# A hybrid attention layer on one core: the mixers' table of steps, reordered over 240 positions

## The chip, the cores and the metric

The kernel runs on one core of one Trainium2 chip. The metric is the device time of one execution in microseconds (us). Three runs of the kernel before the change took 1100.43, 1100.59 and 1101.66 us, so their median is 1100.59 us. One more execution was profiled: it took 1101.76 us, and its span from the first to the last recorded instruction is 1100.0 us. All durations below come from that one.

## The reference

One decoder layer on 512 tokens of width 1024, in float32:

```
h  = x + 1/2 * SwiGLU_1(RMSNorm(x))                  # feed-forward width 2816
u  = RMSNorm(h);  columns of u @ w_in (1024 x 3992): q, k, v of two attentions, branch gates, two merge gates
A  = native sparse attention: compressed keys + selected blocks + window 512; 8 heads of 64, 2 key/value groups
B  = sliding-window attention, window 128, 8 heads, one key/value group, one sink per head
h  = h + w_out( sigmoid(gA) * (A @ w_branch_a) + sigmoid(gB) * (B @ w_branch_b) )
h  = h + 1/2 * SwiGLU_2(RMSNorm(h));  out = RMSNorm(h)
```

The compressed keys and values are a small network over blocks of 32 tokens, `gelu(block @ w1) @ w2`, one for keys and one for values.

## The kernel before, in words

Every large product keeps its precision by splitting both operands into a high part (rounded to the fast matmul type) and a low part (what is left), and by adding three products: high x high, high x low, low x high. So each block of weights, 128 x 1024 numbers that the SP queue loads into `raw`, passes through ScalarE (ACT), which writes `whi` (line 151), and then through VectorE (DVE) or GpSimd (POOL), which writes `wlo` = raw - whi (line 155). Four blocks of `raw` and four of `whi`/`wlo` exist at a time; the load of a block four places ahead is issued behind the second half of a block's low part.

The program runs in stages: the first feed-forward net, the two mixers (attentions A and B), the merge, the second feed-forward net, the last norm. Only the mixers are touched. There the program is cut into 1123 small tasks, in `plan`. Each task is a handful of instructions on one engine:

- `project`: one of 8 groups of six matmuls (line 387, `acc`) that fill one of two accumulator banks with a piece of u @ w_in. What drains the bank (rope on DVE, lines 1166 and 1169; value halves on ACT and DVE, line 1231) sets it free.
- `rope_tasks`, `q_done`, `kv_done`: rotation of queries and keys. Two DVE passes from the bank, an add of the two halves (line 1184, DVE or POOL), then for queries a high part on ACT (line 1260), a low part (line 1263, DVE or POOL), and four transposes on TensorE (line 1272, `tp`), copied out by ACT (line 1277).
- `compress`: four groups of matmuls, a sum on DVE (line 1374), `sums` on TensorE, a polynomial on DVE (lines 1387 to 1389), tanh on ACT, a product on DVE (line 1396), a second product on TensorE (`second`, line 387 `tp<-w,sqacc`), and so on.
- `attend`: for each unit of 128 queries, scores on TensorE (`s`), mask and minimum on DVE (line 1551, with a small add in line 1555), exponentials on ACT (line 1559), the inverse of the sums on DVE (a small add in line 1568 and a reciprocal in line 1569), the weighting (line 1580, DVE or POOL), transposes on TensorE (line 1645), their high part on ACT (line 1657) and low part on DVE (line 1660), the value products, and the sum of two halves (line 1688).
- `prepare`: the high (line 151) and low (line 155) half of a block of weights; the low one on DVE or POOL.

`follow` (in `Schedule`) walks through the table `ORDER`, a list of task numbers, and lets each task write its instructions. Each engine then executes its own instructions strictly in that order and waits by semaphores for what the others make; no engine passes over a waiting instruction. For a task that may run on DVE or POOL, a `p` behind its number puts it on POOL. At every 64th position of the table (63, 127, 191, 255 in the part concerned) `follow` also issues one DMA on POOL's queue, which sums weights for the second feed-forward net in memory. So the table fixes three things: the order on TensorE, ACT, DVE and POOL, which of DVE and POOL does a task, and where POOL's DMAs and SP's loads of weights stand.

Of the kernel before, what the change touches and what calls it, by code (L numbers as in the profile page):

```python
# [207 lines left out]
def cols(w, width, r0, nk, c0, n):  # L208
# [4 lines left out]


ORDER = """
    0 1 2 3 4 5 6 7 14 15 16 10 11p 13 17 32 8 18 36 33 19 37 20 9 21 34 12 44 38 40 80 48 35 41 49 42 23 22 50 39p
    24 26 51 52 25p 53 43p 27 86 54 84 55 45 64 29 82 65 46 30 66 81 85 83p 67 56 57p 68 69 28 31 47 58 87 70 71 59
    72 88 93 95 94p 96 89 60 61 62 90 97 98 91 99 489 100 101 133 134 102 137 135 73 138 139 136 103 104 92 74 63
    140p 105 490 106 75p 502 107 503 108 117 78 491 109 118 76 119 77 492 504 110 507 120 111 493 121 112 122 505 79
    494 506 495 123 496 113 124 155 157 524 115 161 508 141 142 114 125 497 156p 525 143 159 158p 160p 144 163 145  # L220
    498 195 162 146 164 126 199 147 509 526 165 166 197 196p 200 116 167 168 198p 148 510 169 170 149 150 127 499
    176 128p 151 201 529 172 202p 129 500 173p 152 177 130 131 178 511 153 175 154 179 171 132 512 501 527 180 530
    513 528p 516 181 174 517 514 182 183 531 518 185 208 210 212 209 211 213 546 184 515 203 519 187 186p 204 205
    214 551 520 206 547 216 521 217 248 215p 218 249p 188 252 192 219 220 250 253p 552 522 548 193 221 532 189 254
    549 190 523p 251 207 194 222 553 191 223 255p 232 233 533 534 550p 538 234 554 224 535 568 225p 536 539 537 235
    226 540 541 569 542 555p 236 570 543 237 227 238 571 544 545 556 557 560 239 572 561 256 269 240 257 258 271
    270p 273 558 581 259 309 586 313 228 275 260 562 559 272p 261 311 274p 277 582 229 278 262 563 230 564 231 587
    276p 263 279 280 565 312p 281 241p 310p 573 583 603 264 282 574 588 265 584 314p 283 608 266 604 267 605 284
    585p 268 290 291 315 316p 566 285 567p 589 292 575 609 610 606 576 242 286 243p 577 293 294 288 295 611 296 578
    590 244 607 579 246 245 297 360 247 298 591 580 317 595 592 612 299 625 630 318 301 596 287p 289 300p 593 319  # L230
    597 626 302 303 594 306 598 304 307 627 599 305 308 320 613 631 321 614 349 617 618 322 632 600 615 619 323 601
    324 616 602 628 620 325 333 621 334 335 629p 622 633 336 623 326 337 634 338 327 339 635 340 328p 636 329 624p
    350 637 371 330 341 639 640 331 647 342p 332 638 343 641 642 648 656 351 344p 352 657 353 345 643 644 354 649
    347 650 346 665 355 658 651 652 666 348 677 659 356 357 682 653 654 667 660p 668 678 661 645 358 662 655 361 669
    670 663 362 363 664 671 683 672 679 695 684 680 696 364 365 697 685 646p 700 366 701 681p 367 698 686p 687 673
    359 702 368 674 703 713 393 725 691 699p 714 369 688 372 675 689 692 693 373 726 690 370 382 704p 715 705 716
    706 707 730 727 676 694 374 728 729p 709 735 717 708 710 375 711 731 718 719 712 732 376 720 740 736 721 737 741
    733 742 377 722 378 738 757 743 379 739p 758 762 380 734p 759 763 383 384 744p 767 760 745 764 768 746 749 404
    765 772 761p 750 747 385 386 769 770 753 415 748 751 723 754 724p 789 771p 773 752 755 387 774 790 801 756 791
    775 802 766p 806 388 776p 777 781 807 389 803 778 811 390 782 381 792 779 808 785 783 780 812 391 784 804 805p  # L240
    786 793 392 809 813 787 794 394 814 815p 810p 795 816 837 817 788 796 838 395 426 396 797 818 798 397 842 819
    820 839 843 840 847 799 848 800p 821 822 825 398 841p 826 823 399 844 849 829 824 852 827 828 830 833 834 845
    873 400 853 850 854 851p 831 835 832 401 874 846p 855 836 875 856p 885 405 857 406 858 876 859 861 407 865 862
    886 890 860 863 887 866 891 867 869 402 864 888 870 408 871 892 877 895 868 900 896 409 893 897 872 901 921 898
    902 410 878 903 922 411 923 879 926 412 894p 924 416 880 899p 417 904p 931 889 881 905 909 927 882 925p 932 928
    936 906 418 910 419 413 907 911 929 908 930p 933 883 934 913 937 448 914 917 915 912 957 918 420 919 916 437
    935p 938 969 939 958 403 970 421 974 940p 941 920 975 959 960 942 945 971 946 422 943 423 979 949 972 947 976
    977 944 980 950 951 948 984 978p 953 981 427 985 952 982 954 986 961 428 962 1001 429 955 983p 1006 987 956 884p
    988p 963 964 1002 424 973p 1003 965 989 1007 1011 990 430 993 966 1008 991 1012 425 994 1009 431 997 992 998
    1013 432 1016 995 996 1033 1004 999 433 967 1005p 434 1017 1018 1010p 1014 1034 1035 1045 1015p 1019 1020 459  # L250
    1000 1021 1025 968p 1046 1036 1022 1026 438 1023 439 1050 1029 1024 1047 414 1030 1027 1051 1037 1048 1031 1028
    1052 440 1053 1032 1049p 1063 441 1054p 1038 1039 1064 1040 442 1068 435 1041 1065 1042 1055 1069 1056 1059 443
    1060 1066 1070 1057 1061 444 1081 1058 445 1082 481 1093 1067p 449 1071 1083 1072p 1102 1073 1043 1077 1094 1095
    450 451 1084 1062 1103 1074 1096 485 1044p 452 1097p 1078 1075 1111 1085 1104 1079 1112 1105 436 1076 1086 1087
    1106p 1113 1080 1098 453 454 455 1088 1107 446 456 482p 1114 1089 1099 1108 483 1109 460 470 461 462 463 464
    1100 1090 465 1101 1091 1092p 457 486p 466 1115 1110 447 467 1116 487 471 1117 1118 472 1119 484p 488p 1120 1121
    458 473 474 475 476 477 478 479 468 1122p 480 469
"""


# [1894 lines left out]
```

## Time and profile before

| what | value |
|---|---|
| three runs | 1100.43, 1100.59, 1101.66 us |
| profiled execution / its span | 1101.76 / 1100.0 us |
| TensorE busy (PE) | 1085.4 us, 99% of the span |
| VectorE busy (DVE) | 756.5 us, 69% |
| ScalarE busy (ACT) | 526.4 us, 48% |
| GpSimd busy (POOL) | 212.5 us, 19% |
| mean granted TensorE clock | 0.997 |

The mixers' tasks start at 378.6 us of the span; position 60 of the table lies at 398.3 us and position 298 at 460.1 us. In a row of a timeline the first number is the start, the second the duration, and the bracket tells how long the engine was idle before it and what ended that; an "x3" merges equal neighbours. In a row of waits stand the total, the count and the longest. In a row of windows stand, after the stretch, the busy time of PE, PEld, DVE, ACT and POOL with instruction counts, the granted TensorE clock, the DMA share and GB/s.

### The profile page before, as it was taken

How to read it: one execution, taken by the hardware profiler on the slowest of the kernel's cores; microseconds unless marked ns; L12 is line 12 of the kernel's file. 1: busy time of each engine (PE TensorE's matmuls, PEld its weight loads, DVE VectorE, ACT ScalarE, POOL GpSimd, SP SyncE). 2: the span in 40 equal slices, each digit the busy share in tenths (PEclk: the TensorE clock that was granted, in tenths of full speed). 3: DMA queues.
4: the chain of work that ended last, by engine and by line, in shares of the span. 5: the costliest groups of instructions: out<-in, count | busy, mean ns of one | idle time of the engine just before them, and what ended most of it. 6: DMA issues, size and time to landing. Idle time of an engine off the chain costs nothing.

```text
span 1100.0 us, 15779 instructions
## 1 busy us (share of the span) xinstructions
PE 1085.4 (99%) x5835; PEld 934.1 (85%) x5835; DVE 756.5 (69%) x1356; ACT 526.4 (48%) x966; POOL 212.5 (19%) x245
## 2 busy tenths in 40 slices
PE   9999999999999999999999999999999999999997
PEld 7888899988888999998888888888888888888886
DVE  5665778864556578897777657655678867787673
ACT  5433335433334455776767634444335445554442
POOL 0311220000001135565443522122100000000002
PEclk9999999999999999999999999999999999999999
DMA  7989988698756536446969676637998864646622
GB/s 217 259 211 230 250 199 231 207 291 293 229 193 193 143 116 194 153 140 159 301 192 364 149 195 183 191 96 192 245 263 244 264 192 156 191 153 192 211 77 77
DMA packets 203205, 220.90 MB, mean 201 GB/s; under 512 B 7700, under 2 KB 160088, under 8 KB 202840
## 3 DMA queue, kind: packets, MB, share of 16 engines
q1 hardware_dynamic: 177208, 156.84, 45.4%
q0 software_dynamic: 23456, 58.72, 23.2%
q10 hardware_dynamic: 2464, 4.33, 1.1%
q8 instruction: 46, 0.75, 0.3%
q14 instruction: 31, 0.25, 0.1%
HBM read 199.94 MB, written 78.64 MB: 253 GB/s over the span
## 4 chain that ended last, share of the span: by engine, by line
PE 91%; DVE 5%; ACT 1%; issue 1%; DMA 1%; POOLq 0%; ACTq 0%; DVEq 0%
PE acc L387 29%; PE o L387 20%; PE s L387 20%; PE o L1872 4%; PE o L786 3%; PE acc L1872 3%; PE s L1872 3%; PE tp L1645 2%; PE s L786 2%; PE acc L786 2%; DVE wlo L155 1%; DMA raw<-in_ffn_down_dram 1%; DVE s L1551 1%; DVE turn_a L1344 0%; ACT whi L151 0%
## 5 line engine op out<-in xcount | busy, mean ns | idle before, releaser
L155 DVE TENSOR_TENSOR wlo<-raw,whi 128x1024 fp32r<-128x1024 f32 (+2 forms) x219 | 256.5, 1193 | 62.9 <-ACT whi L151 62.4
L151 ACT CAST whi<-raw 128x1024 fp32r<-128x1024 f32 (+2 forms) x244 | 222.0, 935 | 90.0 <-PE acc L387 12.4
L387 PE MATMUL acc<-uh,whi 128*128 128x512 f32 x240 | 96.2, 401 | 0.0
L387 PE MATMUL acc<-uh,wlo 128*128 128x512 f32 x240 | 93.9, 391 | 0.0
L387 PE MATMUL acc<-ul,whi 128*128 128x512 f32 x240 | 93.7, 390 | 0.0
L387 PE MATMUL acc<-whi,uh 128*128 128x256 f32 x224 | 65.9, 294 | 1.3 <-ACT whi L151 1.3
L387 PE MATMUL acc<-wlo,uh 128*128 128x256 f32 x224 | 63.6, 284 | 0.1
L387 PE MATMUL acc<-whi,ul 128*128 128x256 f32 x224 | 63.6, 284 | 0.0
L387 PE MATMUL o<-uh,whi 128*128 128x512 f32 x144 | 57.4, 399 | 0.6 <-ACT whi L930 0.6
L1660 DVE TENSOR_TENSOR pts<-tp,pts 128x512 fp32r<-128x512 f32 (+1 forms) x62 | 41.9, 687 | 22.7 <-ACT pts L1657 21.8
L387 PE MATMUL o<-ul,whi 128*128 128x512 f32 x144 | 56.2, 390 | 0.0
L387 PE MATMUL o<-uh,wlo 128*128 128x512 f32 x144 | 56.1, 390 | 0.0
L387 PEld LDWEIGHTS acc<-uh,wlo 128*128 128x128 f32 x240 | 45.1, 188 | 10.2 <-DVE wlo L155 0.4
L387 PEld LDWEIGHTS acc<-ul,whi 128*128 128x128 f32 x240 | 45.2, 188 | 8.1
L387 PEld LDWEIGHTS acc<-uh,whi 128*128 128x128 f32 x240 | 45.1, 188 | 8.0
L1559 ACT ACTIVATE pbuf<-s,m 128x256 f32<-128x256 f32 (+3 forms) x96 | 47.5, 503 | 8.4 <-DVE m L1551 4.0
L387 PE MATMUL acc<-G,whi 128*128 128x512 f32 x164 | 50.5, 389 | 0.0
L387 PE MATMUL s<-uh,whi 128*128 128x512 f32 x128 | 49.9, 390 | 0.0
L387 PE MATMUL s<-ul,whi 128*128 128x512 f32 x128 | 49.8, 389 | 0.0
L387 PE MATMUL s<-uh,wlo 128*128 128x512 f32 x128 | 49.8, 389 | 0.0
L2050 POOL TENSOR_TENSOR o_t<-o_t,g_b 128x512 f32<-128x512 f32 (+1 forms) x5 | 5.9, 1181 | 227.3 <-ACT z L2044 227.3
L387 PE MATMUL s<-G,whi 128*128 128x512 f32 x160 | 49.4, 390 | 0.0
(468 smaller groups left out, 2923.3 us busy)
## 6 DMA issues: line engine op xcount, KB each, us to landing
raw<-in_ffn_gate_dram SPq DMA_DIRECT2D x42, 512.0 KB, 4.8
raw<-in_ffn_down_dram SPq DMA_DIRECT2D x34, 512.0 KB, 5.1
raw<-in_ffn_up_dram SPq DMA_DIRECT2D x32, 512.0 KB, 6.8
t<-in_ffn_down_dram POOLq DMA_DIRECT2D x12, 1024.0 KB, 9.7
w<-in_ffn_up_dram POOLq DMA_DIRECT2D x12, 1024.0 KB, 11.5
raw<-w SPq DMA_DIRECT2D x24, 512.0 KB, 4.2
raw<-in_w_in_dram SPq DMA_DIRECT2D x20, 512.0 KB, 4.5
raw<-s SPq DMA_DIRECT2D x16, 512.0 KB, 4.9
```

Source lines behind the costliest of these rows:

```text
L151: self.nc.scalar.copy(self.place(i)[0][:, k0:k1], self.raw[i][:, k0:k1])
L155: engine.tensor_tensor(lo, self.raw[i][:, k0:k1], f32(hi), op=OP.subtract)
L387: tensor.matmul(out, lhsT, rhs, start=start, stop=stop)
L786: tensor.matmul(o, a_[:, n], x(k), start=new and n == step == 0, stop=n == 7 and step == 2, skip_group_check=True)
L1551: vector.tensor_tensor_reduce(b.view[:, j], b.view[:, j], u.mask, 1.0, u.least(hd), OP.add, OP.min, u.m[:, hd:hd + 1])
L1559: scalar.activation(u.p[:, hd], b.view[:, j], AF.Exp, bias=u.m[:, hd:hd + 1], scale=-1.0, accum_out=u.sum[:, hd:hd + 1])
L1645: tensor.transpose(ps[:w, hd], u.p[:, hd, kb * w:kb * w + w], ident)
L1660: vector.tensor_tensor(p.lo, flat(b.ps)[:w], f32(p.hi), op=OP.subtract)
L1872: tensor.matmul(ps, x, y[:, k], start=new and kk == k == step == 0, stop=kk == k == 1 and step == 2, skip_group_check=True)
L2050: gpsimd.tensor_tensor(y, y, left["g_b"][:, cs], op=OP.mult)
```

## The change

Positions 60 to 297 of `ORDER` are written anew; all before and behind is the same. The same tasks stand there, none is added or removed, and TensorE and ACT get the same 90 and 62 tasks in another order. 19 tasks change between DVE and POOL: 12 go to POOL (seven low halves of weights in line 155; one low part in line 1350; one in line 1263; two weightings of two heads in line 1580; one output low part in line 1693), and 7 go to DVE (two low halves of weights, three rope adds in line 1184, two weightings). DVE has 59 tasks there instead of 64, POOL 27 instead of 22. The table takes one line more, so that every later line number is one larger in the changed kernel. The diff, cut to its first lines:

```diff
-    24 26 51 52 25p 53 43p 27 86 54 84 55 45 64 29 82 65 46 30 66 81 85 83p 67 56 57p 68 69 28 31 47 58 87 70 71 59
-    72 88 93 95 94p 96 89 60 61 62 90 97 98 91 99 489 100 101 133 134 102 137 135 73 138 139 136 103 104 92 74 63
...
+    39p 24 26 51 52 25p 53 43p 27 86 54 84 55 45 64 29 82 65 46 30 66 28 83 81p 56 85p 87 67 68 57 69 70 31 58
+    59 71 93 60 61 47p 62 88 63 72 89 90 73 91 489 94p 95 74 96 101 102 92 97 98 502 75p 99 100 76 77 103 104
...
```

Three places show how the instructions move. The first is DVE at position 60, from the last piece of the compression's input (line 1344, shown as the first row) to the low part of the first query (line 1263), which TensorE's transposes in line 1272 wait for. Before:

```order
L1344 TENSOR_TENSOR turn_a<-tp,cols_c 64x8x31 x4
L155 TENSOR_TENSOR wlo<-raw,whi 128x512 x2
L1166 TENSOR_TENSOR turn_a<-acc,cos 128x512
L1169 TENSOR_TENSOR turn_b<-acc,sin 128x8x32 x2
L1314 TENSOR_SCALAR gate<-gate 128x96
L1315 RECIPROCAL gate<-gate 128x96
L1195 SCALAR_TENSOR_TENSOR ks_t<-tp,ks_t 128x512
L1350 TENSOR_TENSOR G<-turn_a,G 128x16x32
L155 TENSOR_TENSOR wlo<-raw,whi 128x512
L1263 TENSOR_TENSOR ql<-turn_a,ql 128x8x64
```

and in the changed kernel:

```order
L1345 TENSOR_TENSOR turn_a<-tp,cols_c 64x8x31 x4
L1315 TENSOR_SCALAR gate<-gate 128x96
L1316 RECIPROCAL gate<-gate 128x96
L155 TENSOR_TENSOR wlo<-raw,whi 128x512
L1167 TENSOR_TENSOR turn_a<-acc,cos 128x512
L1170 TENSOR_TENSOR turn_b<-acc,sin 128x8x32 x2
L155 TENSOR_TENSOR wlo<-raw,whi 128x512
L1185 TENSOR_TENSOR turn_a<-turn_a,turn_b 128x512
L1196 SCALAR_TENSOR_TENSOR ks_t<-tp,ks_t 128x512
L1264 TENSOR_TENSOR ql<-turn_a,ql 128x8x64
```

One low half and the low part of line 1350 have left DVE for POOL, and the rope add of line 1184 has come to it from there. On POOL the low half, the DMA and the rope add that stood here have become a low half, the DMA, a second low half and the low part. On TensorE the transposes now stand right behind the projection's last group, ahead of the first two groups of the compression, which stood ahead of them.

The second place is DVE between the compression's polynomial (its last row is line 1389, in the changed kernel 1390) and its product (line 1396, now 1397), which TensorE's second product waits for. Before:

```order
L1389 SCALAR_TENSOR_TENSOR sqacc<-sqacc,tp 128x128
L155 TENSOR_TENSOR wlo<-raw,whi 128x512
L1568 TENSOR_TENSOR sum<-sum,e 128x2
L1569 RECIPROCAL c<-sum 128x2
L1396 SCALAR_TENSOR_TENSOR sqacc<-sqacc 128x128
```

and in the changed kernel, from the low half on:

```order
L155 TENSOR_TENSOR wlo<-raw,whi 128x512
L1185 TENSOR_TENSOR turn_a<-turn_a,turn_b 128x512
L1569 TENSOR_TENSOR sum<-sum,e 128x2
L1570 RECIPROCAL c<-sum 128x2
L1552 ISA s,m<-s,mask_s,sink 128x256
L1552 ISA m 128x1
L1552 ISA s,m<-s,mask_s,sink 128x256
L1552 ISA m 128x1
L1556 TENSOR_TENSOR e<-m,sink 128x2
L1397 SCALAR_TENSOR_TENSOR sqacc<-sqacc 128x128
```

The low half here belongs to another half of the weights than the one before (that one is now on POOL); a rope add and the minima of two heads have come between, and two more heads' minima stand between polynomial and low half (not shown).

The third place is DVE behind the rope passes over the first half of the second key/value projection (lines 1166 and 1169). Before:

```order
L1169 TENSOR_TENSOR turn_b<-acc,sin 128x4x32 x2
L155 TENSOR_TENSOR wlo<-raw,whi 128x512 x3
L1231 SCALAR_TENSOR_TENSOR v<-acc,rcol,v 128x2x64 x2
L1551 ISA s,m<-s,mask_s,sink 128x256
L1551 ISA m 128x1
```

and in the changed kernel:

```order
L1170 TENSOR_TENSOR turn_b<-acc,sin 128x4x32 x2
L1552 ISA s,m<-s,mask_s,sink 128x256
L1552 ISA m 128x1
L1552 ISA s,m<-s,mask_s,sink 128x256
L1552 ISA m 128x1
L1556 TENSOR_TENSOR e<-m,sink 128x2
L1232 SCALAR_TENSOR_TENSOR v<-acc,rcol,v 128x2x64 x2
L155 TENSOR_TENSOR wlo<-raw,whi 128x512 x3
```

The value halves (line 1231), which free the accumulator bank, now stand ahead of the three low halves, with the minima of two heads ahead of them.

More of the change, by code (lines that the diff above doesn't have):

```diff
@@ L221 @@
[L221 to L255, printed above, removed]
@@ L256 @@
-    1100 1090 465 1101 1091 1092p 457 486p 466 1115 1110 447 467 1116 487 471 1117 1118 472 1119 484p 488p 1120 1121
-    458 473 474 475 476 477 478 479 468 1122p 480 469
+    0 1 2 3 4 5 6 7 14 15 16 10 11p 13 17 32 8 18 36 33 19 37 20 9 21 34 12 44 38 40 80 48 35 41 49 42 23 22 50
+    39p 24 26 51 52 25p 53 43p 27 86 54 84 55 45 64 29 82 65 46 30 66 28 83 81p 56 85p 87 67 68 57 69 70 31 58
+    59 71 93 60 61 47p 62 88 63 72 89 90 73 91 489 94p 95 74 96 101 102 92 97 98 502 75p 99 100 76 77 103 104
@@ new lines @@
+    139 78 105 106 107 108 117 490 491 492 493 79 133 135 503 134p 137 507 118 508 509 136 494 504 119 120 121
+    122 123 109 495 110 111 124 155 496 125 138p 140p 159 141 142 143 144 145 505 157 112p 113 114 524 146 529
+    161 497 156p 158p 147 148 160p 530 162 115 126 127 116 195 506p 510 199 163 164 201 165 166 167 168 525 169
+    531 511p 149 150 197 170 151 172 173 171 174 512 513 514 196p 526 152 153 154 498 176 177 178 179 532 128p
+    129 499 130 533 516 517 180 181 182 518 175 198p 527 528 500 183 185 210 203 184 208 546 200p 547 202p 186p
@@ new lines @@
+    204 205 206 131 551 212 188 132 515 519 211p 207 214 534 187 209 216 248 189 249p 254 213 215 217 218 535
+    536 250 251p 219 552 501p 190 538 220 221 191 222 223 232 548 549 553 252 550 537 520 521 522 523p 224 225
+    554 253p 255p 192 193 194 233 234 539 568 235 226 540 541 569 542 555p 236 570 543 237 227 238 571 544 545
+    556 557 560 239 572 561 256 269 240 257 258 271 270p 273 558 581 259 309 586 313 228 275 260 562 559 272p
+    261 311 274p 277 582 229 278 262 563 230 564 231 587 276p 263 279 280 565 312p 281 241p 310p 573 583 603 264
@@ new lines @@
+    282 574 588 265 584 314p 283 608 266 604 267 605 284 585p 268 290 291 315 316p 566 285 567p 589 292 575 609
+    610 606 576 242 286 243p 577 293 294 288 295 611 296 578 590 244 607 579 246 245 297 360 247 298 591 580 317
+    595 592 612 299 625 630 318 301 596 287p 289 300p 593 319 597 626 302 303 594 306 598 304 307 627 599 305
+    308 320 613 631 321 614 349 617 618 322 632 600 615 619 323 601 324 616 602 628 620 325 333 621 334 335 629p
+    622 633 336 623 326 337 634 338 327 339 635 340 328p 636 329 624p 350 637 371 330 341 639 640 331 647 342p
@@ new lines @@
+    332 638 343 641 642 648 656 351 344p 352 657 353 345 643 644 354 649 347 650 346 665 355 658 651 652 666 348
+    677 659 356 357 682 653 654 667 660p 668 678 661 645 358 662 655 361 669 670 663 362 363 664 671 683 672 679
+    695 684 680 696 364 365 697 685 646p 700 366 701 681p 367 698 686p 687 673 359 702 368 674 703 713 393 725
+    691 699p 714 369 688 372 675 689 692 693 373 726 690 370 382 704p 715 705 716 706 707 730 727 676 694 374
+    728 729p 709 735 717 708 710 375 711 731 718 719 712 732 376 720 740 736 721 737 741 733 742 377 722 378 738
@@ new lines @@
+    757 743 379 739p 758 762 380 734p 759 763 383 384 744p 767 760 745 764 768 746 749 404 765 772 761p 750 747
+    385 386 769 770 753 415 748 751 723 754 724p 789 771p 773 752 755 387 774 790 801 756 791 775 802 766p 806
+    388 776p 777 781 807 389 803 778 811 390 782 381 792 779 808 785 783 780 812 391 784 804 805p 786 793 392
+    809 813 787 794 394 814 815p 810p 795 816 837 817 788 796 838 395 426 396 797 818 798 397 842 819 820 839
+    843 840 847 799 848 800p 821 822 825 398 841p 826 823 399 844 849 829 824 852 827 828 830 833 834 845 873
@@ new lines @@
+    400 853 850 854 851p 831 835 832 401 874 846p 855 836 875 856p 885 405 857 406 858 876 859 861 407 865 862
+    886 890 860 863 887 866 891 867 869 402 864 888 870 408 871 892 877 895 868 900 896 409 893 897 872 901 921
+    898 902 410 878 903 922 411 923 879 926 412 894p 924 416 880 899p 417 904p 931 889 881 905 909 927 882 925p
+    932 928 936 906 418 910 419 413 907 911 929 908 930p 933 883 934 913 937 448 914 917 915 912 957 918 420 919
+    916 437 935p 938 969 939 958 403 970 421 974 940p 941 920 975 959 960 942 945 971 946 422 943 423 979 949
@@ new lines @@
+    972 947 976 977 944 980 950 951 948 984 978p 953 981 427 985 952 982 954 986 961 428 962 1001 429 955 983p
+    1006 987 956 884p 988p 963 964 1002 424 973p 1003 965 989 1007 1011 990 430 993 966 1008 991 1012 425 994
+    1009 431 997 992 998 1013 432 1016 995 996 1033 1004 999 433 967 1005p 434 1017 1018 1010p 1014 1034 1035
+    1045 1015p 1019 1020 459 1000 1021 1025 968p 1046 1036 1022 1026 438 1023 439 1050 1029 1024 1047 414 1030
+    1027 1051 1037 1048 1031 1028 1052 440 1053 1032 1049p 1063 441 1054p 1038 1039 1064 1040 442 1068 435 1041
@@ new lines @@
+    1065 1042 1055 1069 1056 1059 443 1060 1066 1070 1057 1061 444 1081 1058 445 1082 481 1093 1067p 449 1071
+    1083 1072p 1102 1073 1043 1077 1094 1095 450 451 1084 1062 1103 1074 1096 485 1044p 452 1097p 1078 1075 1111
+    1085 1104 1079 1112 1105 436 1076 1086 1087 1106p 1113 1080 1098 453 454 455 1088 1107 446 456 482p 1114
+    1089 1099 1108 483 1109 460 470 461 462 463 464 1100 1090 465 1101 1091 1092p 457 486p 466 1115 1110 447 467
+    1116 487 471 1117 1118 472 1119 484p 488p 1120 1121 458 473 474 475 476 477 478 479 468 1122p 480 469
```

3 lines of the change are left out of this document (removed).

## Prediction

> **What bounds the kernel now.** I read the page's first and fourth parts, TensorE's waits, the windows of the stretch that the change touches, and the timelines around each stop of TensorE there.
>
> ```profile
> PE 1085.4 (99%) x5835; PEld 934.1 (85%) x5835; DVE 756.5 (69%) x1356; ACT 526.4 (48%) x966; POOL 212.5 (19%) x245
> PE 91%; DVE 5%; ACT 1%; issue 1%; DMA 1%; POOLq 0%; ACTq 0%; DVEq 0%
> PE tp L387 <- issue: 1.8, 1, 1.8
> PE acc L387 <- ACT whi L151: 1.3, 1, 1.3
> PE tp L1272 <- DVE ql L1263: 0.5, 1, 0.5
> 397.50:460.00 62.50, 58.80 (x477) 57.40 (x477) 55.34 (x139) 38.61 (x103) 32.72 (x30) 0.97 0.62 186
> 431.70:435.10 3.40, 1.61 (x15) 1.37 (x14) 3.29 (x9) 0.41 (x1) 1.63 (x2) 1.00 0.93 303
> 435.10:438.60 3.50, 3.50 (x21) 3.27 (x19) 2.84 (x14) 1.95 (x6) 1.48 (x2) 0.51 0.97 294
> 445.30:448.70 3.40, 2.46 (x19) 2.17 (x17) 3.40 (x5) 3.38 (x9) 3.32 (x4) 1.00 0.00 0
> ```
>
> TensorE is the bound everywhere, and an order takes no matmul away. What it can win is TensorE's idle time in 397.5 to 460 us: 62.50 - 58.80 = 3.7 us, in three stops (0.5, 1.8, 1.3) and 0.1 besides. One thing more hangs on them: behind the stop of 1.8 us the clock row reads 0.51 for 3.5 us. DVE is the second bound in this stretch, busy 55.34 of 62.50 us, so whoever stops TensorE is DVE's queue.
>
> **Why TensorE stops.** These are the stops, and DVE's and POOL's rows around them:
>
> ```profile
> 403.63 0.28 PE L387 MATMUL acc<-whi,ul 128*128 128x256 f32 x1
> 404.60 0.28 PE L387 MATMUL acc<-wlo,G 128*128 128x256 f32 x1
> 405.39 0.88 PE L1272 MATMUL tp<-ident_r,ql 128*128 128x128 f32 x8 [0.52 <-DVE ql L1263]
> 431.78 0.28 PE L387 MATMUL acc<-whi,ul 128*128 128x256 f32 x1
> 433.85 0.42 PE L387 MATMUL tp<-w,sqacc 128*64 128x64 f32 x4 [1.79 <-issue]
> 447.48 0.28 PE L387 MATMUL acc<-wlo,G 128*128 128x256 f32 x1
> 449.02 0.35 PE L387 MATMUL acc<-whi,uh 128*128 128x256 f32 x1 [1.26 <-ACT whi L151]
> 430.59 2.76 DVE L1568 TENSOR_TENSOR sum<-sum,e 128x2 f32<-128x2 f32 x1
> 433.48 0.27 DVE L1396 SCALAR_TENSOR_TENSOR sqacc<-sqacc 128x128 f32<-128x128 f32 x1
> 444.82 3.53 DVE L155 TENSOR_TENSOR wlo<-raw,whi 128x512 fp32r<-128x512 f32 x3
> 448.27 0.60 DVE L1231 SCALAR_TENSOR_TENSOR v<-acc,rcol,v 128x128 fp32r<-128x128 f32 x2
> 430.70 1.42 POOL L1263 TENSOR_TENSOR ql<-turn_a,ql 128x512 fp32r<-128x512 f32 x1
> 431.95 1.38 POOL L155 TENSOR_TENSOR wlo<-raw,whi 128x512 fp32r<-128x512 f32 x1
> 419.30 0.15 DVE L1568 TENSOR_TENSOR sum<-sum,e 128x2 f32<-128x2 f32 x1
> 404.05 0.69 DVE L155 TENSOR_TENSOR wlo<-raw,whi 128x512 fp32r<-128x512 f32 x1
> L1568 DVE TENSOR_TENSOR sum<-sum,e 128x2 f32<-128x2 f32 x6 | 3.5, 588 | 0.1
> ```
>
> A sum of two numbers per row takes 0.15 us alone and 2.76 us while POOL runs two operations (588 ns in the mean of the six in this stretch); a low half takes 0.69 alone and 3.53 / 3 = 1.18 in the run of three. [...] So the product in line 1396 came 2.6 us late and TensorE stood for 1.79. The stop at 449.02 is named after ACT, but the bank that this group writes is freed by line 1231, which ended at 448.27 + 0.60 = 448.87 behind the three low halves.
>
> Start to start a stop costs a little more than its idle time, since matmuls follow each other every 0.12 us: 405.39 - 404.60 - 0.12 = 0.67; 433.85 - 431.78 - 0.12 = 1.95; 449.02 - 447.48 - 0.12 = 1.42. Together 4.04 us.
>
> [...] The row of 2.76 us shows a wait for two; if that were the rule, it would give 1103.5, the rival of the port.
>
> **The clock.** The row at 0.51 is 3.5 us long. The runs shown lie at 1100.43, 1100.59 and 1101.66, the profiled one at 1101.76: two pairs about 1.2 us apart. I read this as runs without and with the slow stretch, and take 1.2 us for it. The median, 1100.59, then has none: the profiled execution stands 1.17 us above it. The stop of 1.26 us (2.46 busy of 3.40) did not slow the clock, that of 1.79 (1.61 of 3.40) did.
>
> [...]
>
> **The change, part by part.** Net, five tasks leave DVE for POOL. [...] What that is worth is decided at the places where TensorE would stand. The times of the changed kernel here are my estimates, each engine's new list followed by these pitches:
>
> ```profile
> 396.27 1.30 POOL L1350 TENSOR_TENSOR G<-turn_a,G 128x512 fp32r<-128x512 f32 x1
> 400.10 0.72 POOL L401 DMA_DIRECT2D w<-in_ffn_gate_dram  x1
> 397.12 1.16 DVE L1344 TENSOR_TENSOR turn_a<-tp,cols_c 64x248 f32<-64x248 f32 x3
> 400.73 0.69 DVE L1166 TENSOR_TENSOR turn_a<-acc,cos 128x512 f32<-128x512 f32 x1
> 402.00 0.20 DVE L1314 TENSOR_SCALAR gate<-gate 128x96 f32<-128x96 f32 x1
> 402.91 0.63 DVE L1195 SCALAR_TENSOR_TENSOR ks_t<-tp,ks_t 128x512 fp32r<-128x512 f32 x1
> 403.45 0.68 DVE L1350 TENSOR_TENSOR G<-turn_a,G 128x512 fp32r<-128x512 f32 x1
> 404.65 0.69 DVE L1263 TENSOR_TENSOR ql<-turn_a,ql 128x512 fp32r<-128x512 f32 x1
> 425.66 1.28 POOL L155 TENSOR_TENSOR wlo<-raw,whi 128x512 fp32r<-128x512 f32 x1 [0.21 <-ACT whi L151]
> 424.15 0.48 DVE L1551 CUSTOM_DVE_ANT_0 s<-s,mask_s,sink 128x256 f32<-128x256 f32 x1
> 425.31 0.16 DVE L1555 TENSOR_TENSOR e<-m,sink 128x2 f32<-128x2 f32 x1
> 425.75 1.74 DVE L155 TENSOR_TENSOR wlo<-raw,whi 128x512 fp32r<-128x512 f32 x1
> 428.01 0.28 DVE L1387 TENSOR_SCALAR sqacc<-tp 128x128 f32<-128x128 f32 x1
> 428.65 0.29 DVE L1389 SCALAR_TENSOR_TENSOR sqacc<-sqacc,tp 128x128 f32<-128x128 f32 x1
> ```
>
> *First stop (line 1272).* DVE is free at 397.12 + 1.16 = 398.28. Its new list: gate 402.91 - 402.00 = 0.91 (to 399.19), low half 0.60 (399.8), rope 1.27 (401.06), low half 0.60, rope add 0.60, ks_t 0.54, query part 0.69. Unhindered that ends at 403.5. But POOL, free at 396.27 + 1.30 = 397.57, now runs a low half to 398.9, its DMA 0.72 to 399.6, a second low half, held by DVE's, to 401.0, and the part of line 1350 to 402.3. DVE's second low half, at 401.06, waits for the latter, 1.25 us. The query part ends at 404.85, and TensorE, whose last projection group ends its pitch at 403.75 as before, starts the transposes at 404.9: a stop of 1.15 instead of 0.67, **+0.5 us**. Behind the waiting transposes stands all of TensorE. Bounds: -0.65 without the port wait (403.8), +1.75 if DVE loses the port twice.
>
> *Second stop (line 1396).* By TensorE's pitches (0.72 per projection group, 0.3 to 0.5 per turn or score group) the second product comes at 432.2. The product needs polynomial, tanh, low half, rope add, sum and two pairs of minima: done near 431.1. **-1.95 us**, with 1.1 to spare. Only that spare covers it.
>
> *A new one.* The low half shown at the second place in the order is the first for which projection groups of the first key/value block wait. Its chain on DVE: a sum that meets three low halves in a row on POOL (1.28 each, 423 to 426.8) at 424.6 and ends with the second at 425.55; reciprocal 0.2; polynomial 428.65 + 0.29 - 428.01 = 0.93; a pair of minima 425.31 + 0.16 - 424.15 = 1.32; low half 0.69: 428.7. TensorE comes at 428.0: **+0.65 us**, between 0 (sum free) and 2.0 (sum held by two operations).
>
> *Third stop (line 1231).* The value halves now go ahead of the low halves, one of which is on POOL, and TensorE has five more small groups to do first. Low halves ready near 444.4, TensorE there at 445.2: **-1.42 us**, spare 0.8.
>
> *The rest.* The 0.1 us at 427 was the wait for a low half of 1.74 us and goes: **-0.1**. Transposes, scores and value products keep their number, so bubbles between kinds of work stay. SP's loads of weights move with the low halves that free their buffers. ACT waited for one once in this stretch, in the row below, and TensorE did not stop for it: high halves are made well ahead of their projections. The tightest now is the load behind POOL's last pair of low halves, some 4 us later against its use; hidden by that lead I take it at nothing, without it at up to 2 us. POOL's four DMAs, 0.72 us each, keep their positions. From position 298 on the order is the old one, and the three rows of waits are all that TensorE has of over 0.4 us between 380 and 700 us, so a gain passes on.
>
> ```profile
> ACT whi L151 <- DMA raw<-in_cmp_k_w_dram: 1.0, 1, 1.0
> ```
>
> **Sum.** -1.95 - 1.42 - 0.1 + 0.5 + 0.65 = -2.3 us. Against the profiled execution: 1101.76 - 2.3 - 1.2 (clock) = 1098.3. Against the median, which I take to be without the slow clock: 1100.59 - 2.3 = 1098.3. I take 1098.2, since a median may hold a share of it.
>
> **Rivals.**
> *Stops only move.* Six more places have a spare of 0.3 to 0.8 us by my estimates, and DVE stays loaded (55.34 - 3.5 of 62.5 us). If four of them miss by 0.5, the gain is 0.3: 1100.3. For it: a low half that moved to POOL takes 1.28 instead of 0.69 us. Against it: DVE's own list is shorter.
> *The port, slower.* POOL's operations follow each other without a gap at three places (three low halves, then two weightings; three low halves later; the pair at position 62). If DVE loses the port to two operations each time, as the 2.76 us row did, instead of one: first stop +1.75, new stop +1.3, a rope add and a sum near 435 +0.9 beyond their spare, and a first stop of 2.9 us slows the clock, +1.2: 1098.3 + 5.15 = 1103.5. It decides from two operations at all three. Against it: the low half at 425.75 waited for one, POOL's of 425.66 (426.94, and DVE was done at 427.49), as the three of 444.82 did by their mean.
> *No new stop.* The sum and the low half meet a free port: 1100.59 - 1.95 - 1.42 - 0.1 - 0.65 = 1096.5.
>
> **Chances.** Forecast 0.60 (1097 to 1099.6 by itself), no new stop 0.14, stops only move 0.16, port 0.10. About 0.2% (2.2 us) is what a measurement of this kernel can tell from no change; the forecast lies on that edge, and a median of the kernel before that holds the slow clock would put the forecast beyond it, so I give 0.40 of its 0.60 to faster. Faster 0.40 + 0.14 = 0.54; within 0.2% 0.20 + 0.16 = 0.36; slower 0.10. Range: from a little under the case without new stops to the moved stops and some of the port: 1096.2 to 1100.9.
>
> **What would show it.** Right: no idle time of over 0.3 us ahead of the second product and of the group behind line 1231, a granted clock of 1.00 over the whole stretch, a stop of about 1.1 us ahead of line 1273, one of about 0.6 ahead of a projection group near 428, and the sum's mean (line 1569 there) well under 588 ns. Wrong: stops of over 0.5 us at other places between 405 and 456, or TensorE waiting behind position 298.

## The result and the profile after

The changed kernel is slower. Six executions took 1106.88 to 1113.38 us, median 1110.03 us; six of the kernel before had a median of 1101.06 us. The ratio is 1.0080, with a 95% interval of 1.0056 to 1.0104. The profiled execution took 1106.92 us (span 1105.2 us), so it is among the shortest of the six; what can be said of the other 3 us of the median stands with the experiments.

TensorE's waits of the changed kernel between 380 and 700 us, all of over 0.3 us (engine, operation and line, what it waited for: total, count, longest):

```profile
PE tp L1422 <- DVE sqacc L1415: 5.1, 1, 5.1
PE tp L1273 <- DVE ql L1264: 2.7, 1, 2.7
PE o L388 <- DVE pts L1661: 0.7, 1, 0.7
```

Two of the three stops of before are gone, and the first has grown from 0.52 to 2.7 us. A stop of 5.1 us is new. It lies ahead of the transposes in line 1422, one step behind the second product that the prediction watched: `second`, a turn on DVE (lines 1411 to 1415), then these transposes. The second product (at 433.81) and the group behind the value halves (at 454.38) are not in the list, so TensorE did not wait for them. What held the other two is in DVE's timeline, with POOL's beside it:

```profile
399.66 3.01 DVE L155 TENSOR_TENSOR wlo<-raw,whi 128x512 fp32r<-128x512 f32 x1
...
434.74 5.69 DVE L1414 TENSOR_TENSOR sqacc<-sqacc 64x64 f32<-64x64 f32 x1
440.47 0.18 DVE L1415 COPY sqacc<-sqacc 64x64 f32<-64x64 f32 x1
...
398.83 0.72 POOL L402 DMA_DIRECT2D w<-in_ffn_gate_dram  x1
399.56 1.31 POOL L155 TENSOR_TENSOR wlo<-raw,whi 128x512 fp32r<-128x512 f32 x1
400.81 1.30 POOL L1351 TENSOR_TENSOR G<-turn_a,G 128x512 fp32r<-128x512 f32 x1
...
433.43 0.74 POOL L402 DMA_DIRECT2D t<-in_ffn_down_dram  x1
434.13 1.36 POOL L155 TENSOR_TENSOR wlo<-raw,whi 128x512 fp32r<-128x512 f32 x1
435.38 1.32 POOL L1264 TENSOR_TENSOR ql<-turn_a,ql 128x512 fp32r<-128x512 f32 x1
436.60 3.74 POOL L155 TENSOR_TENSOR wlo<-raw,whi 128x512 fp32r<-128x512 f32 x3
```

The low half at 399.66 (0.69 us alone) was held until POOL's two operations had ended, at 400.81 + 1.30 = 402.11. The 64 x 64 add in line 1414 (the first expectation below calls it a multiplication), which had taken 0.22 us (line 1413 of the kernel before, in the fence below), was held through five POOL operations, to 436.60 + 3.74 = 440.34.

```profile
434.98 0.22 DVE L1413 TENSOR_TENSOR sqacc<-sqacc 64x64 f32<-64x64 f32 x1
```

Both times a DMA stands on POOL's queue right ahead of the operations. In other places of the same trace a DVE operation was through after a single POOL operation, though POOL went on without a gap, as this sum was, in 0.52 us, while three low halves ran on POOL (to lose or to get the port, as the prediction calls it, means no more than such waits and their ends, which is all that the traces show):

```profile
426.34 0.52 DVE L1569 TENSOR_TENSOR sum<-sum,e 128x2 f32<-128x2 f32 x1
425.55 3.79 POOL L155 TENSOR_TENSOR wlo<-raw,whi 128x512 fp32r<-128x512 f32 x3
```

These windows show where the time went. They are windows of the kernel before and of the changed one, from the same start to where position 298 of the table begins, and three more of the changed kernel (after the stretch: busy time of PE, PEld, DVE, ACT and POOL, granted clock, DMA share, GB/s):

```profile
397.50:460.08 62.58, 58.88 (x477) 57.44 (x477) 55.42 (x140) 38.69 (x103) 32.80 (x30) 0.97 0.62 186
```

```profile
397.50:465.00 67.50, 59.63 (x479) 58.21 (x477) 55.05 (x130) 38.53 (x103) 36.97 (x34) 0.95 0.53 157
435.88:439.30 3.42, 0.00 (x0) 0.00 (x0) 3.42 (x1) 0.00 (x0) 3.42 (x4) 1.00 0.69 265
439.30:442.71 3.41, 2.00 (x9) 1.89 (x10) 3.04 (x9) 1.24 (x4) 1.04 (x1) 0.50 0.62 176
442.71:446.13 3.42, 3.42 (x18) 3.42 (x17) 2.54 (x9) 1.57 (x7) 0.00 (x0) 0.50 0.47 136
```

The stretch is 67.50 - 62.58 = 4.92 us longer. TensorE's idle time went from 62.58 - 58.88 = 3.70 to 67.50 - 59.63 = 7.87 us, 4.17 more, and its busy time grew by 59.63 - 58.88 = 0.75. Most likely that is the clock: behind the stop it is 0.50 for two windows, where matmuls of one kind follow each other every 0.21 us instead of 0.12, with 2.00 + 3.42 = 5.4 us of work in them, against 3.5 us in the kernel before, and half of the difference, by estimate the loss, is 1.0 us. The spans differ by 1105.2 - 1100.0 = 5.2 us; the other 0.3 lie behind position 298, where the changed kernel has the wait of 0.7 us at line 1661, which the kernel before does not have.

### The profile page after: what moved, and what is told of

The parts are those of the page before. It is cut to its first block, busy times and chain, and to the rows that moved or that the text cites. A ratio compares the mean times of both kernels' runs of the same rounds, so it can differ in the third digit from the quotient of the medians.

```text
span 1105.2 us, 15772 instructions
## 1 busy us (share of the span) xinstructions
PE 1086.4 (98%) x5835; PEld 935.4 (85%) x5835; DVE 758.1 (69%) x1351; ACT 525.7 (48%) x966; POOL 217.6 (20%) x250
## 4 chain that ended last, share of the span: by engine, by line
PE 94%; DVE 4%; ACT 1%; issue 1%; POOLq 0%; ACTq 0%; DVEq 0%
PE acc L388 31%; PE o L388 21%; PE s L388 20%; PE o L1873 4%; PE o L787 3%; PE acc L1873 3%; PE s L1873 3%; PE tp L1646 2%; PE s L787 2%; PE acc L787 2%; DVE wlo L155 1%; PE tp L388 1%; DVE sqacc L1414 1%; DVE turn_a L1345 0%; PE tp L1273 0%
## 5 line engine op out<-in xcount | busy, mean ns | idle before, releaser
L155 DVE TENSOR_TENSOR wlo<-raw,whi 128x1024 fp32r<-128x1024 f32 (+2 forms) x214 | 251.3, 1195 | 61.7 <-ACT whi L151 61.2
```

The source lines that it names most:

```text
L155: engine.tensor_tensor(lo, self.raw[i][:, k0:k1], f32(hi), op=OP.subtract)
```

## The experiments

**Theory.** DVE loses the port not to one POOL operation, and not to any run of them, but to a whole run when that run stands right behind a DMA that POOL issues (called a transfer here). **Rivals**: any run of POOL operations without a gap starves DVE; or chance decides. Each kernel below is the changed kernel unless said otherwise; what is not in the edit stays as it is. The places of the transfers in the table are set by one line of `follow`.

| kernel | median us (executions) | ratio to before, 95% |
|---|---|---|
| before, beside these runs | 1101.27 (31), 1101.03 (11), 1101.02 (13) | |
| three transfers moved | 1099.20 (10) | 0.9991 (0.9979 to 1.0002) |
| one transfer moved | 1103.25 (10) | 1.0025 (1.0010 to 1.0040) |
| before, one transfer moved | 1099.79 (10) | 0.9987 (0.9975 to 0.9998) |
| a transfer put ahead of three low halves | 1101.01 (10) | 1.0003 (0.9993 to 1.0012) |
| a transfer put into a run of eight | 1107.09 (4) | 1.0059 (1.0038 to 1.0080) |
| a transfer behind two of the five | 1104.88 (6) | 1.0045 (1.0028 to 1.0062) |
| changed kernel again | 1108.76 (4) | 1.0070 (1.0055 to 1.0085) |
| three moved, two tasks more | 1097.46 (6) | 0.9972 (0.9960 to 0.9984) |
| the same, gates later | 1098.04 (9) | 0.9980 (0.9971 to 0.9990) |

### Three transfers moved into POOL's idle time

```diff
-            if n % 64 == 63 if n < 512 else n % 38 == 37:
+            if n in (82, 146, 235, 255, 319, 383, 447, 511) if n < 512 else n % 38 == 37:
```

> The changed kernel with its order and engines as they are; only three of the transfers that POOL issues (those at positions 63, 127 and 191 of the table) are issued at positions 82, 146 and 235 instead, where POOL stands idle for 2 us or more. Nothing else moves. Theory (a transfer issued by POOL right ahead of operations that follow each other without a gap makes DVE lose the port until that run of POOL's ends): the multiplication of 64 x 64 in line 1414, 5.69 us in the changed kernel, now waits for at most one POOL operation (under 1.6 us), the stop ahead of line 1422 goes from 5.10 to under 0.5, the stop ahead of line 1273 from 2.69 to about 1 us, and the slow clock of 6.8 us goes: 1106.9 - 5.1 - 1.7 - 2.7 = about 1097.4 us. Rival 1 (any run of POOL operations without a gap starves DVE, a transfer or none; the length of the run decides): line 1414 still waits to the end of the run of five, which starts 0.7 us earlier: 4.9 us, a stop of about 4.4, and 1105 to 1106 us. Rival 2 (chance decides who gets the port): somewhere between, with executions that differ by several us.

Measured: 1099.20 us, 11 us under the changed kernel and 2 us under the one before, the latter not clear of noise (0.9979 to 1.0002). Seven of the ten executions lie between 1098.98 and 1099.48 us; the other three took 1100.38 to 1103.61 and have no profile. DVE and POOL in this kernel's timelines:

```profile
399.70 1.02 DVE L155 TENSOR_TENSOR wlo<-raw,whi 128x512 fp32r<-128x512 f32 x1
433.40 0.67 DVE L1414 TENSOR_TENSOR sqacc<-sqacc 64x64 f32<-64x64 f32 x1
434.10 1.16 DVE L1415 COPY sqacc<-sqacc 64x64 f32<-64x64 f32 x1
...
431.45 1.29 POOL L155 TENSOR_TENSOR wlo<-raw,whi 128x512 fp32r<-128x512 f32 x1
432.70 1.29 POOL L1264 TENSOR_TENSOR ql<-turn_a,ql 128x512 fp32r<-128x512 f32 x1
433.94 3.94 POOL L155 TENSOR_TENSOR wlo<-raw,whi 128x512 fp32r<-128x512 f32 x3
437.83 0.77 POOL L402 DMA_DIRECT2D t<-in_ffn_down_dram  x1
```

The same five POOL operations follow each other without a gap, and line 1414 waits for one of them: 0.67 us instead of 5.69. The low half at the first stop takes 1.02 instead of 3.01. So a run alone does not starve DVE, and the first rival falls. The theory's time was 1.8 us too low. Line 1415's copy lost the port once more (1.16 us for 0.18), which leaves a stop of 1.05, and with TensorE earlier by 2 us the low half near 428 is late by 0.7 (TensorE's waits; a fourth of 0.7 us, at line 1661, is as in the changed kernel):

```profile
PE tp L1422 <- DVE sqacc L1415: 1.1, 1, 1.1
PE tp L1273 <- DVE ql L1264: 0.7, 1, 0.7
PE acc L388 <- DVE wlo L155: 0.7, 1, 0.7
```

### One transfer moved, the one ahead of the run of five

```diff
+            if n in (63, 127, 235, 255, 319, 383, 447, 511) if n < 512 else n % 38 == 37:
```

> The changed kernel with one transfer of POOL's moved, the one at position 191, which stood ahead of the run of five, to position 235 behind that run. Theory: line 1414 waits for one POOL operation at most, the stop ahead of line 1422 and the slow clock go, the stop of 2.69 us ahead of line 1273 stays, since the transfer at position 63 stays: 1106.9 - 5.1 - 2.7 = about 1099.1 us. Rival 1 (any run starves DVE): 1105 to 1106 us, with a stop of about 4.4 us ahead of line 1422.

Measured: 1103.25 us, 4 us more than expected. The profiled execution, at 1109.53 us, is the longest of the ten and has a stop of 2.2 us near 600 that no other profile has; its first stretch can be read:

```profile
PE tp L1273 <- DVE ql L1264: 2.7, 1, 2.7
PE tp L1422 <- DVE sqacc L1415: 1.7, 1, 1.7
...
437.69 1.28 DVE L1414 TENSOR_TENSOR sqacc<-sqacc 64x64 f32<-64x64 f32 x1
```

The transfer that stayed keeps its stop (2.7 us), the one that went takes its stop along (5.1 to 1.7, with line 1414 at 1.28 us, one operation). The expectation left out two things. Line 1415's copy lost the port once more, as in the kernel above (1.16 us again), so that 1.7 us of the stop stayed. And the clock ran at half behind both stops in this execution, for 6.8 us behind the one of 2.7 and for 3.4 us behind the one of 1.7.

### The kernel before, with its transfer moved

```diff
-            if n % 64 == 63 if n < 512 else n % 38 == 37:
+            if n in (63, 127, 199, 255, 319, 383, 447, 511) if n < 512 else n % 38 == 37:
```

> The kernel before with one transfer of POOL's moved, from position 191 to 199, so that it stands behind the two POOL operations that held the sum of line 1568 for 2.76 us instead of ahead of them. Theory: the sum waits for one operation (about 1.0 us), the product of line 1396 is ready in time, and the stop of 1.79 us ahead of the second product falls to under 0.3, the slow clock with it: 1101.76 - 1.8 - 1.2 = about 1098.7 us for an execution like the profiled one, so 2 us faster than the median before. Rival 1 (any run of POOL's starves DVE): the run starts 0.7 us earlier and ends 0.7 earlier, the stop is 1.1, and the time 1100.0.

Measured: 1099.79 us, 1.5 us faster than before. The sum that took 2.76 us takes 1.25, but then the product loses the port once as well:

```profile
430.79 1.25 DVE L1568 TENSOR_TENSOR sum<-sum,e 128x2 f32<-128x2 f32 x1
432.16 1.24 DVE L1396 SCALAR_TENSOR_TENSOR sqacc<-sqacc 128x128 f32<-128x128 f32 x1
...
430.29 1.73 POOL L1263 TENSOR_TENSOR ql<-turn_a,ql 128x512 fp32r<-128x512 f32 x1
431.99 1.26 POOL L155 TENSOR_TENSOR wlo<-raw,whi 128x512 fp32r<-128x512 f32 x1
```

So the stop falls from 1.79 to 1.2, not to 0.3, and TensorE's clock stays whole (0.999 in the mean of the execution, 0.997 before). Stop and time are what rival 1 gave (1.1 us and 1100.0), so they do not decide. The rows do decide: rival 1 holds the sum to the end of POOL's run, 431.99 + 1.26 = 433.25, and it was through at 430.79 + 1.25 = 432.04, right behind the first of the two operations. The theory holds for the wait, and its size for the stop was wrong: here two DVE operations in a row each lost one operation's time (1.25 us for 0.15, 1.24 for 0.27).

### A transfer put ahead of three low halves

```diff
+            if n in (82, 157, 235, 255, 319, 383, 447, 511) if n < 512 else n % 38 == 37:
```

> As the first of these kernels (no transfer of POOL's ahead of a run), but the transfer that stood at position 127 is issued at 157, right ahead of the three low halves on POOL at 425.55 us, during which the sum of line 1569 was served after one operation (0.52 us) in the changed kernel. Theory: the sum, at 426.34 us, now waits until the three low halves have ended, some 3.7 us; the low half behind it on DVE comes 3 us late and TensorE stops for about 3 us near 430, 2.5 to 5 us slower than the first of these kernels (with or without a slow clock behind the stop). Rival 1 (any run starves DVE, and a transfer is only 0.7 us of POOL's time): the sum waits for at most one operation as before, and the time is within 1 us of the first of these kernels.

Measured: 1101.01 us, 1.8 us above the kernel with the three moved, which stands for the same code without this transfer there. The sum that was served after one operation in the changed kernel is now held to the run's end (423.59 + 3.77 = 427.36):

```profile
424.40 2.99 DVE L1569 TENSOR_TENSOR sum<-sum,e 128x2 f32<-128x2 f32 x1
...
422.94 0.64 POOL L402 DMA_DIRECT2D w<-in_ffn_gate_dram  x1
423.59 3.77 POOL L155 TENSOR_TENSOR wlo<-raw,whi 128x512 fp32r<-128x512 f32 x3
```

In the kernel with the three moved the same sum took 1.14 us and the same stop was 0.7. The effect can be put in and taken out with nothing but the transfer's place. The time rose by 1.8 us (1.4 between the profiled executions) instead of the 2.5 to 5 expected: the stop was 2.2, not 3, and the clock stayed whole (1.00 from 426.24 to 433.06).

### A transfer inside a run of eight

```diff
+            if n in (82, 146, 235, 255, 335, 383, 447, 511) if n < 512 else n % 38 == 37:
```

> As the kernel with the three transfers moved into idle time, and one more transfer of POOL's moved, from position 319 to 335, so that it stands behind the first low half of POOL's run of eight operations (464.26 to 474.3 us in that kernel) instead of before the run's idle time. There the maxima of line 1556 (two numbers a row) were served after one operation (0.18 and 0.56 us). The first of them now arrives during the second or third POOL operation behind the transfer, not the first. Theory in its strict form (behind a transfer DVE has lost the port until the run ends, however far on): line 1556 waits some 7 us, to about 475, TensorE stops for several us near 470, and the time is 1104 to 1108 us. Theory in its weak form (only who asks during the first operation behind a transfer has lost): line 1556 waits for one operation at most (under 1.3 us), and the time is 1099 to 1100 us. Rival (a transfer makes no difference): as the weak form.

Measured: 1107.09 us, 8 us more than the kernel with the three moved. The strict form holds:

```profile
465.40 0.68 POOL L402 DMA_DIRECT2D w<-in_ffn_up_dram  x1
466.09 5.04 POOL L155 TENSOR_TENSOR wlo<-raw,whi 128x512 fp32r<-128x512 f32 x4
471.09 1.28 POOL L1185 TENSOR_TENSOR turn_a<-turn_a,turn_b 128x512 f32<-128x512 f32 x1
472.34 2.47 POOL L155 TENSOR_TENSOR wlo<-raw,whi 128x512 fp32r<-128x512 f32 x2
...
467.80 7.03 DVE L1556 TENSOR_TENSOR e<-m,sink 128x2 f32<-128x2 f32 x1
```

The small add of line 1556 (two numbers a row; the expectation calls it a maximum) asked for the port in the second operation behind the transfer and got it 7 us later, at 474.81, when POOL's run ended. A wait of one operation would have ended near 468.6 (466.09 + two of 1.26). TensorE stopped for 3.6 and then for 0.5 us and ran 3.4 us at half clock (0.50 from 477.20 to 480.61) behind that, a loss of 1.7 by estimate: together 5.8 of the 6.2 us between the two profiled executions (1105.37 and 1099.16).

### The transfer behind two of the five operations

```diff
+            if n in (82, 146, 215, 255, 319, 383, 447, 511) if n < 512 else n % 38 == 37:
```

> As the kernel with the three transfers moved into idle time, but the one from position 191 goes to 215, between the second and the third of the five operations. Theory (a transfer itself holds no port, but the operations right behind it keep the port): the copy of line 1415, 1.16 us there, falls on the transfer and takes 0.2, the stop ahead of line 1422 goes from 1.05 to about 0.1, and the rope add of line 1185 at 435, 0.71 us there, now waits for all three low halves behind the transfer, about 3.4 us; what TensorE wins at line 1422 it loses within the next 10 us: 1099 to 1101 us. Rival (the run's length decides): copy 1.2 us, rope add under 1.5, 1099.2 us as before.

Measured: 1104.88 us, 3.9 us above the theory's range. The expectation fell in one point: the copy, which fell on the transfer, was not served during it.

```profile
434.23 4.36 DVE L1415 COPY sqacc<-sqacc 64x64 f32<-64x64 f32 x1
...
434.06 0.75 POOL L402 DMA_DIRECT2D t<-in_ffn_down_dram  x1
434.76 3.76 POOL L155 TENSOR_TENSOR wlo<-raw,whi 128x512 fp32r<-128x512 f32 x3
```

The copy began 0.17 us into the transfer and was held through it and through all three low halves behind it (434.76 + 3.76 = 438.52). The stop ahead of line 1422 was 4.2 us instead of 0.1, with 3.4 us at half clock behind it (0.50 from 438.40 to 441.81); the rope add came only when the run had ended and did not wait. So this copy had lost already when it began to wait during the transfer. Two rows of the kernel before show that the transfer by itself does not hold the port:

```profile
428.85 1.82 DVE L155 TENSOR_TENSOR wlo<-raw,whi 128x512 fp32r<-128x512 f32 x1
430.06 0.74 POOL L401 DMA_DIRECT2D t<-in_ffn_down_dram  x1
```

This low half had waited for POOL's operation ahead of the transfer (428.83 to 430.12) and then did its 0.6 us while the transfer was being issued. The next DVE operation, the sum of 2.76 us at 430.59, began inside the transfer and was held to the run's end like the copy. The copy reads a single array and was held; the reciprocal of line 1316, which also reads one, was not (in the changed kernel 0.75 us at 398.99, beside the transfer at 398.83, and 0.75 at 399.03 in the kernel with three moved, without one).

### The changed kernel once more

> The changed kernel itself once more, for a second profile and more times. Its executions lay between 1106.88 and 1113.38 us. Theory for this spread (the clock is looked at in fixed windows of 3.4 us, whose place against the program differs from execution to execution; the two stops are the same in each): the stops ahead of lines 1273 and 1422 measure 2.7 and 5.1 us again within 0.1, and the profiled time differs from 1106.9 by what its half-clock windows take: about 3.4 us more if the stop of 2.7 us is followed by 6.8 us of half clock, as it was in the kernel with one transfer moved. Rival (chance in the port): the stops themselves differ by over 0.5 us from the first profile.

Measured: 1108.76 us, the profiled execution 1108.02. The stops are 2.69 and 5.09 us, as before within 0.01, so chance in the port is not what spreads the times. Two windows of this execution and, below them, two of the first one, from either side of the first stop:

```profile
404.98:408.40 3.42, 1.67 (x16) 1.67 (x17) 3.30 (x7) 2.23 (x5) 1.29 (x1) 1.00 0.68 194
408.40:411.81 3.41, 3.41 (x19) 3.41 (x18) 1.36 (x3) 2.34 (x5) 1.28 (x1) 0.50 0.00 0
```

```profile
405.16:408.57 3.41, 1.90 (x18) 1.90 (x19) 3.29 (x7) 2.46 (x5) 1.30 (x1) 1.00 0.68 192
408.57:411.98 3.41, 3.41 (x31) 3.41 (x31) 2.22 (x5) 2.20 (x5) 1.28 (x1) 1.00 0.00 0
```

The same stop of 2.69 us fell into a window with 1.67 us of work left here, and the next ran at half clock; in the first profile 1.90 were left, and the clock stayed whole. By estimate, half of the work at half clock, that is 1.7 us of loss here and none there; in the kernel with one transfer moved it was two windows. Behind the second stop the two windows at half clock held 0.20 + 3.41 us of work here and 2.00 + 3.42 there, 0.9 us less loss. Together this gives 0.8 of the 1.1 us between the two profiled executions; the 3.4 us more that the expectation names for two windows behind the first stop did not come. So the same program varies by some us with the place of the windows. That the median of 1110.03 is made of such cases is what these three profiles suggest; the other executions have no profile.

### Three transfers moved, and two tasks more

```diff
-  148 160p 530 162 115
+  148 160p 162 530 115
-  224 225 554 253p 255p
+  224 225p 554 253p 255p
```

> As the kernel with the three transfers moved into idle time, with two changes at its remaining stops: the low half for which TensorE waits 0.68 us at 428.85 goes ahead of the pair of minima on DVE (two neighbours in the table trade places), and the rope add at 454.95 (1.57 us on DVE, held by POOL's low halves) goes to POOL, where it was in the kernel before. Expected: the stops of 0.68 at 428.85 and of 0.71 at 459.13 go or fall under 0.2, those of 0.71 ahead of line 1273 and 1.05 ahead of line 1422 stay: 1099.2 - 1.4 = 1097.8 us. Rival (stops only move, since DVE meets POOL's operations at another place): 1099 us or more, with a new stop of 0.5 or more between 425 and 470.

Measured: 1097.46 us, 0.28% faster than before (interval 0.16 to 0.40%), the lowest median of all. The edit shown is made to the kernel with three transfers moved. This table was written on one line, so its line numbers are 42 lower; TensorE's only waits between 380 and 700 us are

```profile
PE tp L1231 <- DVE ql L1222: 0.7, 1, 0.7
PE tp L1380 <- DVE sqacc L1373: 0.6, 1, 0.6
```

Both stops aimed at are gone, and no new one came. The one ahead of the transposes behind the compression (line 1422 there, 1380 here) fell from 1.05 to 0.6, which was not expected.

### The same, with the gates later

```diff
-  66 28 83 81p ...  91 489 94p 95 74 96 101
+  66 83 81p ...  91 489 94p 95 74 96 28 101
```

> As the kernel with the two tasks more, with one further edit at its largest remaining stop (0.70 us ahead of the first transposes): the two DVE operations on the gates (0.58 + 0.75 us with the wait for POOL's low half), which the changed kernel puts ahead of the chain to the query part, go behind the low half at 407, where DVE waits for ACT for some 0.9 us; their first reader comes at 415. Expected: the query part is ready 0.7 us or more earlier, the stop ahead of the transposes goes or falls under 0.1, and the time is 1097.5 - 0.7 = 1096.8 us. Rival (the low half that now follows at once meets POOL's operations instead and waits for two of them, one after the other): the stop stays at 0.5 or more and the time at 1097.4 us.

Measured: 1098.04 us, no gain over the kernel without it (intervals overlap, medians 0.6 us apart the wrong way). The rival came near it, though not by one low half that waits twice: the second low half, at 401.16, which had met a free port (0.68 at 401.97), now took 1.67 us behind one POOL operation, and the first stop only fell from 0.7 to 0.5, while the one in the compression rose from 0.6 to 0.9.

## Why the prediction was wrong

The step that failed is the account of DVE between the second product and the value halves: the sum has no term for it, so it stood at nothing, and a stop of 5.10 us lay there. The term of the first stop was too small besides, and both follow from one missing rule, who gets the port behind a transfer.

**Second and third stop: right.** Both went, in the changed kernel and also with three transfers moved, where TensorE comes 1.3 us earlier to the second product: it started at 432.47 there, 1.2 us behind the end of line 1397, where the sum had 432.2 and a spare of 1.1. The sum prices them at 1.95 and 1.42 us.

**First stop: the cause right, the size wrong.** The sum let DVE's second low half wait for one POOL operation and came to a stop of 1.15 us, with +1.75 as the bound for losing twice. It was the first low half that lost, to two operations, 3.01 us, and the stop was 2.69 us. The price of "one operation" came from the row of 1.74 us at 425.75, a POOL operation with no transfer ahead; the row that fitted this place, 2.76 us at 430.59, had a transfer right ahead at 430.06, as the place itself had. Both rows stood in the trace of before, and the transfer between POOL's two operations was even counted, as 0.72 us of POOL's time.

**The new stop near 428: not there, for another reason.** TensorE came to that group 2 us later than the sum had it, because of the first stop. With the first stop short (three transfers moved), it measured 0.7 us against 0.65 forecast.

**The stop that decided: missing.** DVE's list was followed up to the second product and again from the value halves on; the turn between them, lines 1411 to 1415, was left out. In the kernel before, its add had cost 0.22 us (line 1413) and no wait. The change had put five POOL operations behind the transfer at position 191, where two stood before, and they ran from 434.13 to 440.34 us instead of 430.70 to 433.33, so that the turn, near 434.5 us in both kernels, now fell among them. 5.69 us for one operation, and a stop of 5.10, is what the sum lacked.

**The rival of the port** came nearest, at 1103.5 us, and named the port, but not what decides: it let DVE lose to two operations at three places. Losses were of two at the pair at position 62 and of one at the three low halves near 426 us; at the three later low halves they were of five, to an add that was not on the list. The row of 2.76 us was taken as a matter of how often two are lost, when the transfer at 430.06 stood right ahead of it. Its sum has a slip besides: the +1.75 of the first stop already contains the +0.5 of the forecast, so that 1103.0 would follow. In the working of the first stop 403.5 + 1.25 is 404.75, not 404.85; neither changes a conclusion.

**The clock.** The clock of 1.00 over the whole stretch, which the prediction expected, went with stops of 1.2 us at most; the kernel before had kept it behind its stop of 1.26 us. With stops of 2.7 and 5.1 us it ran at half for 6.8 us in one profile and for 3.4 + 6.8 in the other. The price of 1.2 us for 3.5 us at half clock was low: half of the work in them, 1.7 us by estimate, is lost. In the profiles of the kernel before and of the changed one the half clock comes in stretches of 3.41 us (from 435.12) and 6.83 us (from 439.30), and in both its next stretch, at the end of the program (from 1097.30 and 1101.49), begins 662.19 us, 194 times 3.413, behind the start of the first. Of windows of this length at full clock, those with 1.61 us of work (the kernel before, 431.70 to 435.10), with none (the changed kernel, 435.88 to 439.30), with 1.67 and 1.54 (the same once more, from 404.98 and from 435.70), with 1.36 and at most 1.80 (one transfer moved, from 402.91 and, with the 1.80, between 437.00 and 440.46) and with 0.85 (the transfer in the run of eight, from 473.79) were followed by half clock; those with 1.90 (the changed kernel, from 405.16) and 1.93 (a transfer ahead of three low halves, from 426.24) were not, nor was any with more in the profiles of the kernel before and the changed one.

**The rest.** In the rival of moved stops the 3.5 us taken off DVE are five tasks at a low half's 0.69. The part on weight loads and ACT held: no stop of over 0.3 us is theirs. The part on positions from 298 on did not quite. There TensorE waits 0.7 us at line 1661, one of the signs that the prediction named for being wrong, and the kernel before has no such wait. With the rope add of 1.57 us at 462.68 put back on POOL (two tasks more) it is gone.

## What to carry to other kernels

When one engine's operations grow longer while another's run, read from the trace not only how long they wait, but what stands on the other engine's queue ahead of those that they wait for: here a DMA issued from POOL turned a wait for one operation (0.67 us for the 64 x 64 add) into a wait for the whole run behind it (5.69). Issue such DMAs where the engine idles afterwards, and look at every short operation of the waiting engine that a reordering brings beside such a run, also those that cost nothing before. A planner whose cost for a task is one number can't see this: the same 64 x 64 add took 0.22, 0.67, 1.28 and 5.69 us in four of these kernels.

## What the runs showed of the hardware

Behind a transfer on POOL's queue DVE was held to the end of the run: 2.76 us over two operations in the kernel before; 3.01 over two and 5.69 over five in the changed one; 2.99 over three, 7.03 over six and 4.36 over the transfer and three where a transfer was placed for it; and 1.94 over two even with three moved, behind another transfer that had kept its place (line 1556 at 476.92, the transfer at 476.09). Without a transfer right ahead the waits above were to the end of the operation that was running (0.67 for line 1414 and 1.14 for the sum of line 1569 in the kernel with three moved); in the whole profiles of the kernel before and the changed one the only DVE operations that wait for two POOL operations or more have a transfer right ahead (2.76 us before; 3.01, 5.69 and, at 484.66, 1.93 in the changed kernel). With a gap in POOL's work behind the transfer the effect was gone: in the kernel with the three moved the transfer stood 3.8 us of idle time ahead of the run of eight, and the same small add was served at once, in 0.18 us. In the same kernel a gap of 2.8 us (418.88 to 421.71) was enough as well: the sum of 1.14 us in the run behind it waited for one operation.

```profile
459.77 0.68 POOL L402 DMA_DIRECT2D w<-in_ffn_up_dram  x1
464.26 6.29 POOL L155 TENSOR_TENSOR wlo<-raw,whi 128x512 fp32r<-128x512 f32 x5 [3.81 <-ACT whi L151]
...
467.89 0.18 DVE L1556 TENSOR_TENSOR e<-m,sink 128x2 f32<-128x2 f32 x1
```

Without a transfer DVE came in between two POOL operations that followed each other without a gap (0.67 us for line 1414); behind one it came only at the end of the run (5.69 us). Why the transfer does this stays open: no run here looked inside POOL. It is also open whether any other instruction of POOL has the same effect, and whether other runs do: all the runs above are of POOL operations that read two arrays. POOL's weightings, which read one, held DVE less: the sum of the changed kernel at 430.77 took 0.17 us while weightings ran from 429.33 to 433.47, and the add of line 1556 in the kernel with three moved 0.41 instead of 0.16 at 430.63, while they ran from 429.66 to 431.48.
